# Whole token copies from PSUM, one more pair by seven products, and another order of weight sums in a hybrid decoder layer

## The chip, the cores and the metric

The kernel runs on one core of a Trainium2 chip. A core has a matrix engine (TensorE, PE in the profile), a vector engine (VectorE, DVE), a scalar engine (ScalarE, ACT), GpSimd (POOL) and SyncE (SP, which here issues most transfers). Each engine runs its own instructions in order and waits on semaphores for the others. Matmul results go to PSUM, eight banks of 128 x 512 fp32 each; everything else on the chip is in SBUF. The metric is the device time of one execution in microseconds.

## The reference

One layer works on 512 tokens of width 1024 in fp32: a SwiGLU FFN, a token mixer (two kinds of attention), and a second FFN.

```python
def swiglu(x, w_gate, w_up, w_down):
    return (jax.nn.silu(x @ w_gate) * (x @ w_up)) @ w_down
...
        h = rms_norm(x, ffn1_pre[l])
        x = x + 0.5 * rms_norm(swiglu(h, ffn1_w_gate[l], ffn1_w_up[l], ffn1_w_down[l]), ffn1_post[l])
        h = rms_norm(x, mix_pre[l])
        y = token_mixer(h, w_in[l], nsa_pe_k[l], nsa_w_ck1[l], nsa_w_ck2[l], nsa_pe_v[l],
                        nsa_w_cv1[l], nsa_w_cv2[l], w_nsa_o[l], w_dil_o[l], w_mix_out[l])
        x = x + rms_norm(y, mix_post[l])
        h = rms_norm(x, ffn2_pre[l])
        x = x + 0.5 * rms_norm(swiglu(h, ffn2_w_gate[l], ffn2_w_up[l], ffn2_w_down[l]), ffn2_post[l])
```

The hidden width D_FF is 2816, 22 blocks of 128 columns.

## The kernel before, in words

**Numbers.** Every fp32 operand is kept as two parts, `hi` (ACT casts it to a shorter type, L106) and `lo` (DVE subtracts `hi` from it, L107). A product is three matmuls, hi by hi, hi by lo and lo by hi (`mm3`, L129 to L131).

**An FFN.** The normalised tokens stand transposed, as `xh` and `xl`. The 22 blocks of hidden columns are taken in 11 pairs. A pair is worked in one of two ways. A *classical* pair has four units (gate and up, for two blocks), each of 24 matmuls with 512 columns of tokens; per unit, weights of 128 x 1024 come from DRAM into one of three `raw` buffers and are split. A pair by *seven products* (`strassen`) forms, from the four blocks A11, A12, A21, A22 (gate and up for two halves of the model width), sums S1 to S4 on DVE, splits these, and multiplies them with sums T1 to T4 of the tokens or with blocks of tokens: seven block products, each of 24 matmuls with 256 columns. `STRASSEN` says which pairs go that way: 3 to 10 in the first FFN and 2 to 10 in the second.

**Token sums.** T1 to T4 are formed in `token_sums` while the classical pairs run, a few steps (`STEPS`) behind each block. A step first joins `xh` and `xl` into the whole value again (`join`, L493, DVE), subtracts (L496), and splits the result. Slots of SBUF have tags; a step of work can start when the slot's last user is done.

**The norm.** Token tile t (128 tokens) is scaled by DVE (L197), transposed by PE into two PSUM banks (L202), cast from there by ACT to `xh` (L205), and the rest is taken by DVE to `xl` (L209). `norm_steps` gives these as functions. The banks' tags are given by hand: `OPEN` for the first FFN, `AFTER_MIX` for the second. PSUM has three banks S, two T, one V and two F.

**What sets the order.** The opening (in `run`) is issued by hand, in the order of the text, for ACT, DVE and PE: tile 0 goes through two S banks, tile 1 through two T banks, then the first FFN unit starts. The first four units of an FFN work on the first two tiles alone (256 columns); the first two of them write into banks of tag T ("TTSV"), the others into S and V. `keep_busy` issues transposes of no use to keep PE working. Tiles 2 and 3 are transposed between those units. Elsewhere a scheduler orders each engine's instructions, within what the program's data allow.

Of the kernel before, what the change touches and what calls it, by code (L numbers as in the profile page):

```python
# [12 lines left out]
F32 = mybir.dt.float32  # L13
# [14 lines left out]
NF = DFF // P  # L28
# [31 lines left out]
class Layer:  # L60
    def __init__(self, ctx, tc, a):
        self.tc, self.nc, self.a = tc, tc.nc, a
        self.pool = ctx.enter_context(tc.tile_pool(name="sb", bufs=1))
        self.psum = ctx.enter_context(tc.tile_pool(name="ps", bufs=1, space=PSUM))
        self.nps = 0
        self.consts()

# [118 lines left out]

    def norm_steps(self, t, pre, tags):

        nc = self.nc
        xn = self.sbt("tmp", [P, D], bufs=2)  # L190
        c = slice(t * P, (t + 1) * P)
        xh, xl = self.xht, self.xlt
        pt = {}

        def scale(h, r):
            hc = slice(h * S, (h + 1) * S)
            nc.vector.scalar_tensor_tensor(xn[:, hc], self.x[2 * t + h], r, pre[h], op0=OP.mult, op1=OP.mult)  # L197

        def transpose(h):
            pt[h] = self.bank(tags[h])  # L200
            for j in range(4):
                nc.tensor.transpose(pt[h][:, j * P:(j + 1) * P], xn[:, (4 * h + j) * P:(4 * h + j + 1) * P], self.ident)  # L202
# [73 lines left out]
    def ffn(self, n, wg, wu, wd, post, finish, xsrc, tags, nps, aside=None):  # L276
# [48 lines left out]
        def strassen(p):  # L325
# [17 lines left out]
            r12, r21, r11, r7 = [self.bank() for _ in range(4)]  # L343
            nc.vector.tensor_add(s1, a21, a22)
            w = block(a11)
# [44 lines left out]
        def classical(f, act):  # L390
            bs = []
            for m in "gu":
                if (m, f) in first:
                    w, b = first[m, f]
                    mms(w, b, 2 * P, S)
                else:
                    w = unit(m, f)
                    b = self.bank()
                    mms(w, b, 0, S)
                bs.append(b)  # L400
            nc.scalar.activation(act, bs[0], AF.Silu)
# [69 lines left out]
    def token_sums(self):  # L471


        nc = self.nc
        H = S // 2
        places = []
# [5 lines left out]
        for c in range(2):  # L482
            hi, lo, whole = [[v.rearrange("p (k c) -> p k c", k=2) for v in g]
                             for g in (places[8 * c:8 * c + 4], places[8 * c + 4:8 * c + 8],
                                       [self.slot("x") for _ in range(4)])]
            f1, f2, f3, f4 = whole
# [4 lines left out]
            def join(dst, i, h, c=c):  # L491
                ks, cs = slice(4 * i + 2 * c, 4 * i + 2 * c + 2), slice(h * H, (h + 1) * H)
                nc.vector.tensor_add(dst, self.xht[:, ks, cs].bitcast(F32), self.xlt[:, ks, cs].bitcast(F32))  # L493

# [900 lines left out]
    def run(self, out):  # L1395
# [30 lines left out]
        with self.tc.manual_schedule(engines={ET.Activation, ET.DVE, ET.PE}):  # L1426
# [73 lines left out]
        self.mixer(*boundary(a["mix_post"][0], a["ffn2_pre"][0], self.x2dram, AFTER_MIX))  # L1500
        self.ffn(1, a["ffn2_w_gate"][0], a["ffn2_w_up"][0], a["ffn2_w_down"][0],
# [31 lines left out]
```

## Time and profile before

| | us |
|---|---|
| median of 3 runs | 1138.97 (1138.95 to 1139.98) |
| profiled execution | 1138.51 |
| its span | 1136.4 |
| PE busy | 1119.9 (99%) |
| DVE busy | 908.0 (80%) |
| ACT busy | 638.0 (56%) |
| granted clock of PE, mean | 0.999 |

The span runs from the first to the last instruction that the profiler saw. Busy times are sums over the span; in a window they say how full an engine is there. A row of a timeline gives start, duration, engine, line of the program, operation, output and inputs, and in brackets the time that the engine waited before it and for what.

### The profile page before, as it was taken

Reading aid. Unit: us, or ns where it says so; the run is one execution under the profiler, and the core shown is the slowest. Engines: PE = TensorE matmul, PEld = TensorE weight load, DVE = VectorE, ACT = ScalarE, POOL = GpSimd, SP = SyncE. Lnnn points to the kernel's source line nnn. Section 1 sums busy time; section 2 is a strip of 40 time slices with the busy share of each in tenths; the row PEclk is TensorE's granted clock in tenths of the full one; section 3 lists DMA queues with packets and bytes.
Section 4 is the critical chain, followed back from the end, with each engine's and each line's share of the span. In section 5 each row is a group of like instructions: output and inputs, shape, how many; then the busy total and the mean of one; then the engine's idle time right before and its main releaser. Section 6 shows DMA issues by size and latency. Waiting matters only on the chain.

```text
span 1136.4 us, 18463 instructions
## 1 busy us (share of the span) xinstructions
PE 1119.9 (99%) x6921; PEld 999.5 (88%) x6921; DVE 908.0 (80%) x1563; ACT 638.0 (56%) x1145; POOL 78.3 (7%) x112
## 2 busy tenths in 40 slices
PE   8999999999999999999999999999999999999997
PEld 7889999998878987778888998788989999998885
DVE  6989999878667889687665687976878888979665
ACT  5435555566464688687565635644445555558552
POOL 1000000000022032343000000001000000000001
PEclk9999999999999999999999999999999999999999
DMA  9995665578655552111476758683133433357753
GB/s 321 331 307 187 190 199 186 154 265 295 220 184 148 172 134 85 53 41 56 142 248 224 251 176 293 207 301 107 66 121 121 130 98 129 109 181 236 280 189 115
DMA packets 152908, 206.01 MB, mean 181 GB/s; under 512 B 19794, under 2 KB 97906, under 8 KB 152564
## 3 DMA queue, kind: packets, MB, share of 16 engines
q1 hardware_dynamic: 152816, 204.85, 55.1%
q8 instruction: 54, 0.88, 0.3%
q14 instruction: 34, 0.28, 0.1%
q10 hardware_dynamic: 4, 0.00, 0.0%
HBM read 165.45 MB, written 39.37 MB: 180 GB/s over the span
## 4 chain that ended last, share of the span: by engine, by line
PE 88%; DVE 6%; ACT 2%; DMA 1%; issue 1%; POOL 1%; SPq 0%; POOLq 0%; DVEq 0%; ACTq 0%
PE pb_F L131 11%; PE pb_F L129 11%; PE pb_F L130 11%; PE pb_S L131 8%; PE pb_S L130 8%; PE pb_S L129 8%; PE pb_T L130 6%; PE pb_T L131 6%; PE pb_T L129 6%; PE pb_V L130 3%; PE pb_V L129 3%; PE pb_V L131 3%; PE pb_V L986 2%; PE pb_T L971 1%; DVE SP_s L721 1%
## 5 line engine op out<-in xcount | busy, mean ns | idle before, releaser
L106 ACT CAST whi<-raw 128x1024 fp32r<-128x1024 f32 (+2 forms) x221 | 225.4, 1020 | 260.3 <-issue 68.2
L107 DVE TENSOR_TENSOR wlo<-raw,whi 128x1024 fp32r<-128x1024 f32 (+2 forms) x221 | 261.3, 1185 | 103.6 <-ACT whi L106 99.7
L129 PE MATMUL pb_F<-xh_t,whi 128*128 128x512 f32 (+1 forms) x392 | 142.6, 364 | 0.6 <-ACT whi L106 0.4
L131 PE MATMUL pb_F<-xh_t,wlo 128*128 128x512 f32 (+1 forms) x392 | 141.6, 361 | 0.5 <-DVE wlo L107 0.5
L130 PE MATMUL pb_F<-xl_t,whi 128*128 128x512 f32 (+1 forms) x392 | 141.9, 362 | 0.0
L106 ACT CAST whi<-tmp_t 128x1024 fp32r<-128x1024 f32 x51 | 53.5, 1048 | 61.0 <-PE pb_S L130 22.0
L131 PEld LDWEIGHTS pb_F<-xh_t,wlo 128*128 128x128 f32 x392 | 74.1, 189 | 10.8 <-DVE wlo L107 1.0
L129 PEld LDWEIGHTS pb_F<-xh_t,whi 128*128 128x128 f32 x392 | 74.1, 189 | 10.6 <-ACT whi L106 0.6
L130 PEld LDWEIGHTS pb_F<-xl_t,whi 128*128 128x128 f32 x392 | 74.2, 189 | 9.7
L107 DVE TENSOR_TENSOR wlo<-tmp_t,whi 128x1024 fp32r<-128x1024 f32 x51 | 62.4, 1223 | 25.2 <-ACT whi L106 23.9
L129 PE MATMUL pb_S<-xh_t,whi 128*128 128x256 f32 (+1 forms) x240 | 73.2, 305 | 0.0
L131 PE MATMUL pb_S<-xh_t,wlo 128*128 128x256 f32 (+1 forms) x240 | 73.0, 304 | 0.0
L130 PE MATMUL pb_S<-xl_t,whi 128*128 128x256 f32 (+1 forms) x240 | 73.0, 304 | 0.0
L151 POOL TENSOR_TENSOR rs_t<-rs_t,mhalf_t 128x1 f32<-128x1 f32 x24 | 19.2, 798 | 546.4 <-DVE rs_t L147 546.4
L130 PE MATMUL pb_T<-xl_t,whi 128*128 128x256 f32 (+1 forms) x184 | 53.9, 293 | 0.0
L129 PE MATMUL pb_T<-xh_t,whi 128*128 128x256 f32 (+1 forms) x184 | 53.9, 293 | 0.0
L131 PE MATMUL pb_T<-xh_t,wlo 128*128 128x256 f32 (+1 forms) x184 | 53.8, 292 | 0.0
L962 POOL TENSOR_SCALAR SP_s<-SP_s,st_t 128x384 f32<-128x384 f32 (+2 forms) x48 | 45.7, 968 | 106.5 <-DVE st_t L898 80.5
L130 PEld LDWEIGHTS pb_S<-xl_t,whi 128*128 128x128 f32 x240 | 45.9, 191 | 1.9
L129 PEld LDWEIGHTS pb_S<-xh_t,whi 128*128 128x128 f32 x240 | 45.9, 191 | 1.9
L131 PEld LDWEIGHTS pb_S<-xh_t,wlo 128*128 128x128 f32 x240 | 45.9, 191 | 1.9
L107 DVE TENSOR_TENSOR PT_s<-pb_T,PT_s 128x512 fp32r<-128x512 f32 (+1 forms) x72 | 39.2, 559 | 6.1 <-ACT PT_s L106 5.5
(808 smaller groups left out, 3350.6 us busy)
## 6 DMA issues: line engine op xcount, KB each, us to landing
raw<-in_ffn_w_up_dram SPq DMA_DIRECT2D x36, 512.0 KB, 5.2
raw<-in_w_in_dram SPq DMA_DIRECT2D x18, 1024.0 KB, 5.4
raw<-in_ffn_w_gate_dram SPq DMA_DIRECT2D x35, 512.0 KB, 4.7
raw<-tdram SPq DMA_DIRECT2D x16, 1024.0 KB, 5.2
raw<-in_ffn_w_down_dram SPq DMA_DIRECT2D x14, 1024.0 KB, 5.7
NN_s<-in_ffn_w_down_dram SPq DMA_DIRECT2D x22, 512.0 KB, 5.1
tdram<-NN_s SPq DMA_DIRECT2D x22, 512.0 KB, 3.9
raw<-tdram SPq DMA_DIRECT2D x8, 768.0 KB, 5.9
```

Source lines behind the costliest of these rows:

```text
L106: self.last_cast = self.nc.scalar.copy(dsthi, src).ins
L107: self.last_rest = self.nc.vector.tensor_sub(dstlo, src, dsthi.bitcast(F32)).ins
L129: mm(out, lhi, rhi, start=start, stop=False, skip_group_check=skip)
L130: mm(out, lhi, rlo, start=False, stop=False, skip_group_check=skip)
L131: mm(out, llo, rhi, start=False, stop=stop, skip_group_check=skip)
L151: nc.gpsimd.tensor_tensor(out=r, in0=v, in1=self.mhalf, op=OP.pow)
L721: nc.vector.tensor_tensor_reduce(p, s, w, -1.0, FLOOR, OP.add, OP.min, st_m)
L962: nc.gpsimd.tensor_scalar(pp, pp, st[:, 1, t:t + 1], None, op0=OP.mult)
L971: nc.tensor.transpose(b[:, o + (t - kk) * P:o + (t - kk + 1) * P], pt[pn][:, po + kk * P:po + (kk + 1) * P], self.ident)
L986: self.nc.tensor.matmul(out[:, kk * P:S], v, pp, start=first and kk == 0 and pi == 0, stop=False, skip_group_check=True)
```

## The change

1. At the norm, ACT now also copies each transposed bank whole (`full`, four copies of 128 x 2 x 128 per tile), for the token half 0 into slots V and for half 1 into slots x. `token_sums` reads these; the joins of `xh` and `xl` are gone.
2. Pair 2 of the first FFN is worked by seven products. Token sums are thus spread over blocks 1 to 3 in both FFNs, four steps each.
3. The weight sums of such a pair are formed as S3 = A11 - A21, S2 = A22 - S3, S1 = S2 + A11, S4 = A12 - S2, instead of S1, S3, S2, S4. These are four operations on DVE as before.

```diff
-STRASSEN = range(3, NF // 2), range(2, NF // 2)
+STRASSEN = range(2, NF // 2), range(2, NF // 2)
...
-STEPS = (0, 3, 3, 3, 3), (4, 4, 4)
+STEPS = (0, 4, 4, 4), (0, 4, 4, 4)
...
+WHOLE = "VV", "xx"
...
+    def new_whole(self, half):
+        self.whole[half] = [[self.slot(tag).rearrange("p (k c) -> p k c", k=2) for _ in range(2)] for tag in WHOLE[half]]
...
+        def full(h):
+            if not whole:
+                return
+            if t % 2 == 0 and h == 0:
+                self.new_whole(t // 2)
+            for j in range(2):
+                o = self.whole[t // 2][h][j][:, :, (t % 2) * P:(t % 2 + 1) * P]
+                self.last_cast = nc.scalar.copy(o, pt[h][:, 2 * j * P:2 * (j + 1) * P].rearrange("p (j c) -> p j c", j=2)).ins
...
                 transpose(h)
                 cast(h)
                 rest(h)
+            for h in range(2):
+                full(h)
...
-            nc.vector.tensor_add(s1, a21, a22)
             w = block(a11)
             nc.vector.tensor_sub(a21, a11, a21)
             product(r11, w, b11, True, False)
             w = block(a21)
             product(r7, w, t3, True, True)
-            nc.vector.tensor_sub(s2, s1, a11)
+            nc.vector.tensor_sub(s2, a22, a21)
             w = block(s2)
+            nc.vector.tensor_add(s1, s2, a11)
...
-            if f == 1:
+            if f == 0:
                 sums.extend(self.token_sums())
...
-            def s1(f1=f1, f3=f3, join=join):
-                join(f3, 0, 1)
-                join(f1, 0, 0)
+            def s1(f1=f1, f3=f3):
                 sub(f1, f3, f1)
...
+            full0(0)
             sq2 = self.squares(2)
+            full0(1)
             self.pre_split.append(self.ktiles(self.wsplit(self.pre_raw["g"][:, :, P:2 * P], [KT, P])))
-            t2 = self.norm_T(2, g, OPEN[2], sq2)
+            t2 = self.norm_T(2, g, OPEN[2], sq2, True)
+            full1(0)
             sq3 = self.squares(3)
+            full1(1)
             self.pre_split.append(self.wslots(self.pre_raw["u"][:, :, P:2 * P], "SP"))
-            t3 = self.norm_T(3, g, OPEN[3], sq3)
+            t3 = self.norm_T(3, g, OPEN[3], sq3, True)
```

Two places show how instructions move. First, ACT in the opening, from the split of the second unit's weights (`whi_183`) to that of the fourth's (`SP_s`); `pb_S_136` and `pb_S_142` are tile 0's transposes, `pb_T_155` and `pb_T_166` tile 1's, `whi_201` (`whi_193` before) the third unit's weights, `junk_t` the squares. Before:

```order
L106 CAST whi_183<-raw_83 128x1024
L138 ACTIVATE junk_t_187,ss_t_188<-x_s_78 128x512
L138 ACTIVATE junk_t_190,ss_t_191<-x_s_79 128x512
L106 CAST whi_193<-raw_82 128x1024
L138 ACTIVATE junk_t_204,ss_t_205<-x_s_80 128x512
L138 ACTIVATE junk_t_207,ss_t_208<-x_s_81 128x512
L106 CAST SP_s_210<-raw_83 128x512
```

And of the change:

```order
L109 CAST whi_183<-raw_83 128x1024
L224 COPY V_s_187<-pb_S_136 128x2x128
L224 COPY V_s_188<-pb_S_136 128x2x128
L141 ACTIVATE junk_t_193,ss_t_194<-x_s_78 128x512
L141 ACTIVATE junk_t_196,ss_t_197<-x_s_79 128x512
L224 COPY V_s_189<-pb_S_142 128x2x128
L224 COPY V_s_190<-pb_S_142 128x2x128
L109 CAST whi_201<-raw_82 128x1024
L224 COPY V_s_187<-pb_T_155 128x2x128
L224 COPY V_s_188<-pb_T_155 128x2x128
L141 ACTIVATE junk_t_214,ss_t_215<-x_s_80 128x512
L141 ACTIVATE junk_t_217,ss_t_218<-x_s_81 128x512
```

Six copies stand among these splits and squares; those from `pb_T_155` come ninth and tenth in this list. The other side of it is PE's first FFN unit, whose bank has the same tag T (`pb_T_226` before, `pb_T_238` now), before and now:

```order
L129 MATMUL pb_T_226<-xh_t_88,whi_133 128x256 [waits DVE_49]
```

```order
L132 MATMUL pb_T_238<-xh_t_88,whi_133 128x256 [waits DVE_49,Activation_49]
```

The matmul waits for ACT too. Second, DVE at the start of the second FFN, from tile 3's mean square (`rs_t`) through its scale (`tmp_t`) to the rests of tiles 2 and 3. Before:

```order
L147 TENSOR_SCALAR rs_t<-ss_t 128x1
L197 SCALAR_TENSOR_TENSOR tmp_t<-x_s,rs_t,CP_s 128x512 x2
L209 TENSOR_TENSOR xl_t<-pb_F,xh_t 128x4x128 x2
L209 TENSOR_TENSOR xl_t<-pb_S,xh_t 128x4x128
L209 TENSOR_TENSOR xl_t<-pb_V,xh_t 128x4x128
L493 TENSOR_TENSOR x_s<-xh_t,xl_t 128x512 x3
```

And of the change:

```order
L150 TENSOR_SCALAR rs_t<-ss_t 128x1
L362 TENSOR_TENSOR raw<-raw 128x1024
L203 SCALAR_TENSOR_TENSOR tmp_t<-x_s,rs_t,CP_s 128x512 x2
L215 TENSOR_TENSOR xl_t<-pb_F,xh_t 128x4x128 x2
L215 TENSOR_TENSOR xl_t<-pb_S,xh_t 128x4x128
L215 TENSOR_TENSOR xl_t<-pb_V,xh_t 128x4x128
L507 TENSOR_TENSOR V_s<-x_s,V_s 128x512
```

The sum S3 of a pair's weights (`raw<-raw`) now stands ahead of tile 3's scale, and a subtraction of whole copies stands where the joins stood.

More of the change, by code (lines that the diff above doesn't have):

```diff
@@ L65, in __init__ @@
         self.nps = 0
+        self.whole = {}
         self.consts()
@@ L185, in squares, with norm_steps @@
         return [self.meansq(x, S) for x in self.x[2 * t:2 * t + 2]]
-    def norm_steps(self, t, pre, tags):
+    def new_whole(self, half):
+        self.whole[half] = [[self.slot(tag).rearrange("p (k c) -> p k c", k=2) for _ in range(2)] for tag in WHOLE[half]]
+    def norm_steps(self, t, pre, tags, whole=False):
         nc = self.nc
@@ L209, in rest, with norm_T @@
             self.last_rest = nc.vector.tensor_sub(xl[:, ks, c], pt[h].rearrange("p (j c) -> p j c", j=4), xh[:, ks, c].bitcast(F32)).ins
-        return scale, transpose, cast, rest
-    def norm_T(self, t, pre, tags, sq=None):
+        def full(h):
[6 more added lines that the diff above has]
+                self.last_cast = nc.scalar.copy(o, pt[h][:, 2 * j * P:2 * (j + 1) * P].rearrange("p (j c) -> p j c", j=2)).ins
+        return scale, transpose, cast, rest, full
+    def norm_T(self, t, pre, tags, sq=None, whole=False):
         r = self.rstd(sq or self.squares(t))
-        scale, transpose, cast, rest = self.norm_steps(t, pre, tags)
+        scale, transpose, cast, rest, full = self.norm_steps(t, pre, tags, whole)
         for h in range(2):
@@ L402, in classical @@
             nc.vector.tensor_mul(act, act, bs[1])
-            if f == 1:
+            if f == 0:
                 sums.extend(self.token_sums())
-            if 1 <= f <= len(STEPS[n]):
+            if f < len(STEPS[n]):
                 with self.tc.issue_after(self.last_rest):
-                    for _ in range(STEPS[n][f - 1]):
+                    for _ in range(STEPS[n][f]):
                         sums.pop(0)()
@@ L474, in token_sums @@
         nc = self.nc
-        H = S // 2
         places = []
@@ L482, in token_sums @@
         for c in range(2):
[L483 to L486, printed above, removed]
+            hi, lo = [[v.rearrange("p (k c) -> p k c", k=2) for v in g]
+                      for g in (places[8 * c:8 * c + 4], places[8 * c + 4:8 * c + 8])]
+            whole = f1, f2, f3, f4 = [self.whole[h][i][c] for i, h in ((0, 0), (1, 1), (0, 1), (1, 0))]
             for i in range(4):
@@ L489, in token_sums @@
                     o.extend(v[:, k] for k in range(2))
-            def join(dst, i, h, c=c):
-                ks, cs = slice(4 * i + 2 * c, 4 * i + 2 * c + 2), slice(h * H, (h + 1) * H)
-                nc.vector.tensor_add(dst, self.xht[:, ks, cs].bitcast(F32), self.xlt[:, ks, cs].bitcast(F32))
             def sub(dst, x, y):
@@ L499, in parts, with s2, s3 @@
                 self.split(hi[i], lo[i], whole[i])
-            def s1(f1=f1, f3=f3, join=join):
-                join(f3, 0, 1)
-                join(f1, 0, 0)
+            def s1(f1=f1, f3=f3):
                 sub(f1, f3, f1)
-            def s2(f1=f1, f2=f2, f3=f3, join=join):
-                join(f2, 1, 1)
+            def s2(f1=f1, f2=f2, f3=f3):
                 sub(f3, f2, f3)
                 sub(f2, f2, f1)
-            def s3(f2=f2, f4=f4, join=join):
-                join(f4, 1, 0)
+            def s3(f2=f2, f4=f4):
                 sub(f4, f4, f2)
@@ L1440, in run @@
             r0 = self.rstd(sq0)
-            scale0, transpose0, cast0, rest0 = self.norm_steps(0, g, OPEN[0])
-            scale1, transpose1, cast1, rest1 = self.norm_steps(1, g, OPEN[1])
+            scale0, transpose0, cast0, rest0, full0 = self.norm_steps(0, g, OPEN[0], True)
+            scale1, transpose1, cast1, rest1, full1 = self.norm_steps(1, g, OPEN[1], True)
             hi, lo = self.wpair([KT, P])
@@ L1475, in run, with boundary @@
             self.pre_split = [self.ktiles(w) for w in ((hi, lo), self.wsplit(self.pre_raw["u"][:, :, 0:P], [KT, P]))]
+            full0(0)
             sq2 = self.squares(2)
+            full0(1)
             self.pre_split.append(self.ktiles(self.wsplit(self.pre_raw["g"][:, :, P:2 * P], [KT, P])))
-            t2 = self.norm_T(2, g, OPEN[2], sq2)
+            t2 = self.norm_T(2, g, OPEN[2], sq2, True)
+            full1(0)
             sq3 = self.squares(3)
+            full1(1)
             self.pre_split.append(self.wslots(self.pre_raw["u"][:, :, P:2 * P], "SP"))
-            t3 = self.norm_T(3, g, OPEN[3], sq3)
+            t3 = self.norm_T(3, g, OPEN[3], sq3, True)
         self.pending = [t2, t3]
-        def boundary(post, pre, store, tags=None):
+        def boundary(post, pre, store, tags=None, whole=False):
             def load():
@@ L1494, in finish @@
                         self.new_xT()
-                    self.pending.append(self.norm_T(t, gain, tags[t]))
+                    self.pending.append(self.norm_T(t, gain, tags[t], None, whole))
             return load, finish
@@ L1499, in run @@
                  *boundary(a["ffn1_post"][0], a["mix_pre"][0], self.xdram, AFTER_FFN), a["x"][0], "TTSV", 6, self.distances)
-        self.mixer(*boundary(a["mix_post"][0], a["ffn2_pre"][0], self.x2dram, AFTER_MIX))
+        self.mixer(*boundary(a["mix_post"][0], a["ffn2_pre"][0], self.x2dram, AFTER_MIX, True))
         self.ffn(1, a["ffn2_w_gate"][0], a["ffn2_w_up"][0], a["ffn2_w_down"][0],
```

## The prediction

> **What bounds the kernel now.** I read the busy times and the chain of waits first, then busy time by windows over the two FFNs, then TensorE's (PE's) timeline with ScalarE (ACT) and VectorE (DVE) beside it where the diff changes something.
>
> ```profile
> PE 1119.9 (99%) x6921; PEld 999.5 (88%) x6921; DVE 908.0 (80%) x1563; ACT 638.0 (56%) x1145; POOL 78.3 (7%) x112
> ...
> PE 88%; DVE 6%; ACT 2%; DMA 1%; issue 1%; POOL 1%; SPq 0%; POOLq 0%; DVEq 0%; ACTq 0%
> ```
>
> ```profile
> core 0: us, PE busy (x) PEld busy (x) DVE busy (x) ACT busy (x) POOL busy (x), PEclk, DMA share, GB/s
> 12.00:337.00 325.00, 323.91 (x2155) 298.85 (x2154) 280.23 (x370) 175.99 (x255) 6.20 (x14) 1.00 0.71 236
> 780.00:1117.00 337.00, 336.61 (x2299) 312.86 (x2297) 273.31 (x351) 185.00 (x273) 5.41 (x9) 1.00 0.45 149
> ```
>
> PE fills the span, and within the FFNs it misses only 1.09 of 325.00 us and 0.39 of 337.00. So an edit there pays only if PE issues less, and costs only if PE comes to a stop. DVE at 86% of the first window (280.23 of 325.00) is next. My sum has three questions: what the new products save on PE, where a new order stops PE, and whether the clock holds.
>
> **Pair 2 by seven products.** PE's timeline, start and duration of each row:
>
> ```profile
> 76.32 0.39 PE L129 MATMUL pb_V<-xh_t,whi 128*128 128x512 f32 x1
> 81.76 0.28 PE L129 MATMUL pb_S<-xh_t,whi 128*128 128x256 f32 x1
> ...
> 104.79 0.28 PE L129 MATMUL pb_V<-NN_s,whi 128*128 128x256 f32 x1
> 107.67 0.28 PE L129 MATMUL pb_S<-NN_s,whi 128*128 128x256 f32 x1
> ```
>
> The first two rows are the last classical unit of pair 2 and the start of pair 3: 81.76 - 76.32 = 5.44 us for 24 matmuls of 512 columns, 0.227 each. The other two bound one block product: 107.67 - 104.79 = 2.88 us for 24 of 256 columns, 0.12 each. A classical pair is four units, 4 x 5.44 = 21.76; the new one 7 x 2.88 = 20.16. **Saving 1.60 us**: an eighth less work would be 2.72, but 256 columns take 0.12 where half of 0.227 would be 0.114, and 168 x 0.0067 gives 1.1 of it back. Nothing else in the change takes work from PE, so 1.60 us is also all that it can gain.
>
> **The opening: who may write the T banks.** At the start, the first two FFN units write the two T banks of PSUM, which hold tile 1's transposed tokens. Until now these were free once ACT had cast them to xh and DVE had taken xl. Now ACT must copy from them first, and in its order the two copies from the first T bank stand behind two from S, the squares of tile 2, two more from S and the split of a third unit's weights. The issue order shows the new wait on ACT at the first of PE's 256-column matmuls. Rows of before:
>
> ```profile
> 11.43 0.60 PE L1424 MATMUL pb_V<-ident_t 128*128 128x128 f32 x4
> 12.03 0.39 PE L129 MATMUL pb_T<-xh_t,whi 128*128 128x256 f32 x1
> ```
>
> ```profile
> 12.14 1.06 ACT L106 CAST whi<-raw 128x1024 fp32r<-128x1024 f32 x1
> 13.10 0.64 ACT L138 ACTIVATE junk_t<-x_s 128x512 bf16<-128x512 f32 x1
> ...
> 13.86 0.63 ACT L138 ACTIVATE junk_t<-x_s 128x512 bf16<-128x512 f32 x1
> ...
> 15.04 1.05 ACT L106 CAST whi<-raw 128x1024 fp32r<-128x1024 f32 x1 [0.46 <-DMA raw<-in_ffn_w_gate_dram]
> 15.99 0.62 ACT L138 ACTIVATE junk_t<-x_s 128x512 bf16<-128x512 f32 x1
> ```
>
> The copy itself isn't in the trace; the nearest row, ACT out of PSUM with the same 128x256, is this group (busy 11.5 us, mean 370 ns):
>
> ```profile
> L106 ACT CAST PT_s<-pb_T 128x256 fp32r<-128x256 f32 x32 | 11.5, 370 | 7.3 <-DVE PT_s L107 3.8 <-PE pb_T L1237 2.3 <-PE pb_T L971 1.0
> ```
>
> Neighbours on ACT overlap by some 0.1 us: the cast of 1.06 is followed 0.96 later, the square of 0.63 (with its accumulator read) 0.76 later. So a copy advances ACT by 0.28 when another follows. The chain: split 12.14 to 13.10; two copies to 13.66; two squares (0.76 each) to 15.18; two copies to 15.74; the split of 0.95 to 16.69 (its DMA had landed by 15.04); two copies, the last in full, 16.69 + 0.28 + 0.37 = 17.34. With a handover of 0.06, PE's first FFN matmul moves **from 12.03 to about 17.40**. If copies didn't overlap at all (0.37 each), it is 17.85; at 0.22 each 17.1.
>
> The second T bank comes free two squares and two copies later, 17.25 + 1.52 + 0.65 = 19.42; the second unit wants it at 17.40 + 2.88 = 20.28, so it adds no wait. What follows swallows part of the delay:
>
> ```profile
> 18.93 1.31 PE L202 MATMUL pb_S<-ident_t,tmp_t 128*128 128x128 f32 x8 [0.65 <-DVE tmp_t L197]
> ...
> 22.95 1.04 PE L202 MATMUL pb_F<-ident_t,tmp_t 128*128 128x128 f32 x8
> 23.74 0.36 PE L129 MATMUL pb_V<-xh_t,SP_s 128*128 128x256 f32 x1
> ...
> 26.69 0.28 PE L129 MATMUL pb_T<-xh_t,whi 128*128 128x256 f32 x1
> ```
>
> Two units 17.40 + 5.76 = 23.16; tile 2's eight transposes at the 0.79 of the third and second row (23.74 - 22.95), the third unit at 2.95 (26.69 - 23.74), then tile 3's transposes and the fourth unit the same: 23.16 + 2 x (0.79 + 2.95) = 30.64, where 26.69 stood. The opening costs **+3.95 us** (3.6 to 4.4 by the two copy prices); the 0.65 of waiting in the first row is gone, since the scaled tokens are then long there.
>
> **The start of the second FFN.** No bank wait there: AFTER_MIX frees both T banks before units reach them. But in DVE's order a weight sum of 128x1024 (now S3) goes between tile 3's mean square and its scale:
>
> ```profile
> 800.19 0.21 DVE L147 TENSOR_SCALAR rs_t<-ss_t 128x1 f32<-128x1 f32 x1 [0.95 <-ACT junk_t L138]
> 801.13 1.41 DVE L197 SCALAR_TENSOR_TENSOR tmp_t<-x_s,rs_t,CP_s 128x512 f32<-128x512 f32 x2 [0.73 <-POOL rs_t L151]
> ```
>
> ```profile
> 802.03 0.60 PE L202 MATMUL pb_S<-ident_t,tmp_t 128*128 128x128 f32 x4
> 802.60 0.66 PE L202 MATMUL pb_V<-ident_t,tmp_t 128*128 128x128 f32 x4
> ```
>
> DVE sat idle for 0.73 of that; the sum takes about 1.13 (1.22 for one of its size in the row at 73.20 below, less the 0.1 by which neighbours overlap), so it starts at about 800.4 and ends near 801.5, and the scale, PE's transposes behind it and the units behind those come **+0.35 us** later (0, if the order on the chip lets the sum fall elsewhere, to 0.5).
>
> **DVE elsewhere, costed at nothing.** The joins that go are these:
>
> ```profile
> L493 DVE TENSOR_TENSOR x_s<-xh_t,xl_t x16: 681/684/687, 34.9 to 828.8; 128x512 f32<-128x512 f32 x16
> ```
>
> Eight per FFN at some 0.60 spacing leave DVE 4.8 us. A Strassen pair, though, asks more of it than a classical one:
>
> ```profile
> 38.20:60.00 21.80, 21.80 (x99) 18.04 (x97) 21.06 (x35) 6.96 (x10) 1.44 (x2) 1.00 0.90 303
> 60.00:81.80 21.80, 21.80 (x98) 18.06 (x97) 18.14 (x26) 7.49 (x11) 0.00 (x0) 1.00 0.93 313
> 101.90:122.10 20.20, 20.20 (x171) 20.20 (x170) 19.28 (x26) 10.93 (x15) 0.00 (x0) 1.00 0.62 203
> 73.20 1.22 DVE L344 TENSOR_TENSOR tmp_t<-raw 128x1024 f32<-128x1024 f32 x1 [2.00 <-DMA raw<-in_ffn_w_up_dram]
> ```
>
> DVE is busy 19.28 of 20.20 us in such a pair, yet PE is busy for all 20.20. Token sums that were spread over pairs 0 to 2 must now be done by the end of pair 1, in the 21.80 us from 38.20 where DVE already works 21.06; but the joins' 4.8 us go from there, and PE's 4 us of delay in the opening add room before it. ACT has 7 to 11 us of work in each of these windows; 32 copies of 0.28, 9 us over both FFNs, fit. The cover is DVE's lead over PE; without it, each us that DVE is late is a us of PE. The order S3, S2, S1, S4 has four operations like the old; no Strassen pair of before shows PE waiting for a sum, so nothing is there to win. ACT and SP have no other long queue moved past them: V slots come later to the early loads of pair 5, x slots earlier to pairs 3 and 4.
>
> **Sum at full clock:** 1138.51 (the profiled execution; span 1136.4 and 2.1 around it) - 1.60 + 3.95 + 0.35 = 1141.2. The timed runs have their median at 1138.97, 0.46 above the profiled one; measured the same way, that is 1141.7.
>
> **The clock.** PE now idles for 17.40 - 12.03, about 5.4 us. What idling did to the granted clock in this trace shows only at its ends:
>
> ```profile
> 1129.56 0.39 PE L131 MATMUL pb_T<-whi,PT_s 128*128 128x512 f32 x1
> ```
>
> ```profile
> 1133.50:1134.00 0.50, 0.00 (x0) 0.00 (x0) 0.00 (x0) 0.00 (x0) 0.00 (x0) 1.00 0.98 360
> 1134.00:1134.20 0.20, 0.00 (x0) 0.00 (x0) 0.00 (x0) 0.00 (x0) 0.00 (x0) 0.78 1.17 430
> 1134.20:1134.40 0.20, 0.00 (x0) 0.00 (x0) 0.00 (x0) 0.00 (x0) 0.00 (x0) 0.50 0.93 358
> ```
>
> ```profile
> 6.69 1.97 PE L202 MATMUL pb_S<-ident_t,tmp_t 128*128 128x128 f32 x8 [0.41 <-DVE tmp_t L197]
> ...
> 10.42 0.64 PE L1424 MATMUL pb_V<-ident_t 128*128 128x128 f32 x2
> 10.85 0.75 PE L202 MATMUL pb_T<-ident_t,tmp_t 128*128 128x128 f32 x4
> ```
>
> After the last matmul (1129.56 + 0.39 = 1129.95) the clock fell to 0.50 at about 1134.1, 4.2 us later. At the start, two transposes took 0.43 (10.85 - 10.42), 0.215 each, where eight take 0.79 in the row at 22.95, 0.099 each: PE ran at half speed until about 11, 4.3 us after the dense work of 6.69 had begun. A gap of 5.4 us is longer than 4.2, so I take it that PE comes back at half speed and keeps it for up to 4.3 us, in which half the work is lost: 0 to 2.1 us. I take 0.9, below the middle, since the gap passes 4.2 by only 1.2 and the three timed runs need not all be hit: **1142.6**.
>
> The Trainium skill, "TensorE: Matmul & The Clock Gate" (Part 1: The HAM clock gate), says that the gate halves the clock after an idle window of about 3.4 us and restores it after about as much sustained work, with windows that run freely whatever the kernel does. The 4.2 us at the end agree with that. By windows that don't start with the gap, 5.4 us can hold a whole one or not; the page thus speaks for a time that varies between executions, and by its 3.4 us an estimate of the loss would be 1.7 us or none.
>
> **Rivals.**
> (a) The clock stays full: the gap holds no complete stretch that the gate counts. For it: only 1.2 us separate the gap from the 4.2 that it took. From rows alone, the rise near 11 and the fall at 1134.1 are places of such a rhythm, and what lies between them is unknown. Then 1141.7. Chance 0.30. That is the case to which the page's free-running window belongs.
> (b) The banks come free early, and PE starts by about 12.3 as before: ACT would have to come to T's copies ahead of the squares and the splits. ACT works 12.14 to 15.99 with no idle but 0.46, and the order shows the wait, so little speaks for it. Then 1138.97 - 1.60 + 0.35 = 1137.7, not slower. It decides if the first copy out of T starts before 12.3. Chance 0.06.
> (c) DVE's lead is too short: in order as it is, it waits for a weight load (the 2.00 us at 73.20 is one), with the new pair's operands and the token sums queued behind; PE then stops in pair 1 or 2. The same 2.00 us once more on top of the forecast gives 1144.6. Against it: joins gone, and the opening's delay gives DVE 4 us. Chance 0.10.
> The forecast (PE late, half clock for a while) has 0.54.
>
> **How the numbers follow.** A change under 0.2%, 2.28 us here, can't be told from none. The forecast, 1142.6 (1141.2 to 1144.3 by 3.6 to 4.4 in the opening, 0 to 0.5 in the second FFN and 0 to 2.1 of clock, not all at one end), is slower than 1141.25 for nearly all of it: 0.52 of 0.54. Of (a), 0.45 us above that bound, 0.20 of 0.30. (b) is within the bound but for 0.02. (c) is slower. Slower 0.52 + 0.20 + 0.10 = 0.82; same 0.02 + 0.10 + 0.04 = 0.16; faster 0.02. The range, with (a)'s lower half and (c) in it: 1140.6 to 1145.0.
>
> **What would show it.** Right: PE's first 128x256 matmul into pb_T starts at 17.1 to 17.9, released by ACT's copy out of pb_T; transposes of tile 2 follow the second unit without a wait; its 256-column matmuls are 0.2 us or more apart for some us and then 0.12, or 0.12 from the start (a). Pair 2 lasts 20.2 us, with PE filled from 31 to the end of pair 3. Tile 3's scale in the second FFN is 0.3 to 0.4 later in relation to its mean square. Wrong: an FFN start by 12.3; a PE wait for a wlo of 1 us or more in pairs 0 to 3; or a window with the FFN's PE under 99%.

## The result, and the profile after

The changed kernel takes 1149.58 us (median of 4 runs, 1147.91 to 1151.4) against 1139.22 for the kernel before (1138.95 to 1139.98): a ratio of **1.009, interval 1.0075 to 1.0104**, 10.4 us slower. The way was forecast (0.82 for slower), the size was not: 1142.6 in a range to 1145.0. Its profiled execution took 1147.91 us with a span of 1146.1. Of the kernel before, one run beside the first batch below (the change with parts undone) took 2211.0 us and is left out, and one beside the second (one part at a time, and the copies with banks V, S, T, T) took 1154.49 us at a granted clock of 0.927, where its others took 1138.7 to 1141.5, so the intervals of that batch are wide; medians are compared there.

The page of the changed kernel, its busy times and the chain that ended last:

```profile
PE 1121.8 (98%) x6993; PEld 1004.3 (88%) x6993; DVE 906.4 (79%) x1557; ACT 651.6 (57%) x1185; POOL 79.4 (7%) x112
...
PE 76%; DVE 11%; DMA 5%; issue 3%; ACT 3%; POOL 1%; SPq 0%; DVEq 0%; POOLq 0%; ACTq 0%
```

PE does only 1.9 us more work than before, but its share of the chain fell from 88% to 76%; VectorE and transfers took it over. What PE waited for, by line (total, times, longest):

```profile
PE pb_T L132 <- ACT V_s L224: 4.7, 1, 4.7
PE pb_S L1279 <- DVE PT_s L110: 2.2, 2, 1.7
...
PE pb_S L134 <- DVE wlo L110: 0.7, 2, 0.4
```

The first row is the bank wait of the opening. The others are short, and a list by length hides them; they are found by laying the two traces side by side. Both end with the same matmuls, so PE's rows can be counted back from the last one, and the start of each compared. In the table, "+4.71" means that this matmul starts 4.71 us later in its span than the same one before. The columns are places of the kernel before: pair 3's start (81.8 us), the last pairs of the first FFN (214.8), two places around the end of the mixer (704.7 and 746), the second FFN once all tiles are transposed (816.9), and the last matmul.

| run (one profiled execution each) | 81.8 | 214.8 | 704.7 | 746 | 816.9 | last | median of the timed runs, us |
|---|---|---|---|---|---|---|---|
| the change | +4.71 | +7.04 | +7.35 | +8.64 | +9.52 | +9.49 | 1149.58 |
| old sums | +4.37 | +4.38 | +3.89 | +5.31 | +5.36 | +5.39 | 1143.54 |
| banks V, S, T, T | -1.10 | +1.12 | +1.43 | +1.83 | +2.66 | +2.66 | 1141.40 |
| dummies | +3.27 | +5.36 | +5.47 | +5.69 | +6.52 | +6.51 | 1144.84 |
| both edits | -0.99 | -0.98 | -1.36 | -1.34 | -1.31 | -1.27 | 1139.76 |
| before, new sums only | +0.15 | +2.57 | +3.04 | +3.41 | +4.28 | +4.26 | 1141.79 |
| before, pair 2 only | +2.29 | +2.29 | +2.12 | +2.70 | +2.72 | +2.76 | 1143.67 |
| before, copies only | +5.34 | +5.34 | +5.49 | +5.77 | +5.81 | +5.82 | 1144.95 |
| both edits, fewer sums | +0.17 | +0.18 | +0.12 | +0.98 | +1.06 | +1.06 | 1138.72 |
| both edits, four sums on GpSimd | +8.30 | +8.31 | +7.84 | +8.85 | +8.89 | +9.01 | 1148.40 |
| both edits, fewer loads | -0.72 | -0.72 | -1.11 | -0.56 | -0.52 | -0.48 | 1137.38 |
| copies, banks V, S, T, T | -0.17 | -0.17 | +0.27 | +0.29 | +0.33 | +0.37 | 1138.67 |
| both edits, late call | +0.83 | +2.07 | +1.74 | +3.68 | +3.93 | +3.93 | 1139.79 |
| copies, banks V, S, T, T, late call | -0.85 | -0.85 | -0.51 | -0.25 | -0.07 | +0.32 | 1138.49 |

The change's own row reads as a sum. At pair 2's start it is +6.32; pair 2 takes 1.61 off; pairs 3 to 9 add 2.33, of it 1.53 in pair 3; the mixer 1.60, most of it at one place near 710 us; the start of the second FFN 0.88. That place in the mixer differs from run to run (0.0 to 1.9 us between the columns 704.7 and 746, and both ends of that are kernels with the same banks and the same sums, "both edits" without and with the late call): VectorE waits there for a transfer, of the change and of the kernel before:

```profile
717.19 1.23 DVE L110 TENSOR_TENSOR wlo<-raw,whi 128x1024 fp32r<-128x1024 f32 x1 [1.61 <-DMA NN_s<-in_ffn_w_down_dram]
```

```profile
708.58 1.23 DVE L107 TENSOR_TENSOR wlo<-raw,whi 128x1024 fp32r<-128x1024 f32 x1 [0.35 <-DMA NN_s<-in_ffn_w_down_dram]
```

I don't count it to the change; that it has another cause is not shown, since each kernel has one profile.

**The opening.** PE's timeline of the changed kernel, to be held against 12.03 before:

```profile
11.89 1.06 PE L1431 MATMUL pb_V<-ident_t 128*128 128x128 f32 x4
17.66 0.58 PE L132 MATMUL pb_T<-xh_t,whi 128*128 128x256 f32 x1 [4.71 <-ACT V_s L224]
18.04 0.41 PE L133 MATMUL pb_T<-xl_t,whi 128*128 128x256 f32 x1
18.26 0.41 PE L134 MATMUL pb_T<-xh_t,wlo 128*128 128x256 f32 x1
...
22.10 0.35 PE L134 MATMUL pb_T<-xh_t,wlo 128*128 128x256 f32 x1
22.29 0.28 PE L132 MATMUL pb_T<-xh_t,whi 128*128 128x256 f32 x1
22.41 0.28 PE L133 MATMUL pb_T<-xl_t,whi 128*128 128x256 f32 x1
...
25.52 1.04 PE L208 MATMUL pb_S<-ident_t,tmp_t 128*128 128x128 f32 x8
```

ScalarE at the same time:

```profile
13.56 0.65 ACT L224 COPY V_s<-pb_S 128x256 f32<-128x256 f32 x2
14.09 0.65 ACT L141 ACTIVATE junk_t<-x_s 128x512 bf16<-128x512 f32 x1
...
16.01 1.05 ACT L109 CAST whi<-raw 128x1024 fp32r<-128x1024 f32 x1
16.95 0.66 ACT L224 COPY V_s<-pb_T 128x256 f32<-128x256 f32 x2
17.48 0.66 ACT L141 ACTIVATE junk_t<-x_s 128x512 bf16<-128x512 f32 x1
```

The chain is the forecast one, each copy 0.26 behind the last: the two copies from the first T bank end at 16.95 + 0.66 = 17.61, and PE starts at 17.66, released by them. Then its matmuls are 0.213 apart (22 from 17.66 to 22.10) until 22.1, and 0.12 from 22.29 on. In this run the half speed didn't begin in the gap: the four transposes just ahead of it took 1.06 us (11.89), where before they took 0.60 (11.43), so PE hadn't come to full speed yet. Its clock record begins with full speed at 22.25, where that of the kernel before begins at 11.13; ahead of the first entry the profile counts full speed, whatever the spacing. The second T bank causes no wait, nor do tile 2's transposes.

**VectorE in the pairs.** Two neighbours on VectorE, and PE behind them:

```profile
90.75 1.22 DVE L362 TENSOR_TENSOR raw<-raw 128x1024 f32<-128x1024 f32 x1 [2.63 <-DMA raw<-in_ffn_w_up_dram]
91.90 1.22 DVE L110 TENSOR_TENSOR wlo<-tmp_t,whi 128x1024 fp32r<-128x1024 f32 x1
```

```profile
93.17 0.39 PE L134 MATMUL pb_F<-NN_s,wlo 128*128 128x256 f32 x1 [0.54 <-DVE wlo L110]
```

The first is S3 of pair 4 (L362), a pair that PE begins only at 108.2. It waits 2.63 us for its weights. Behind it, in order, stands a split of pair 3, which PE needs at once. So the new sum, early because it needs only one half of the next pair's weights, holds up a split that has all its data.

**The second FFN's start.** VectorE and GpSimd of the changed kernel:

```profile
808.87 0.22 DVE L150 TENSOR_SCALAR rs_t<-ss_t 128x1 f32<-128x1 f32 x1 [0.95 <-ACT junk_t L141]
809.02 1.23 DVE L362 TENSOR_TENSOR raw<-raw 128x1024 f32<-128x1024 f32 x1
810.68 1.41 DVE L203 SCALAR_TENSOR_TENSOR tmp_t<-x_s,rs_t,CP_s 128x512 f32<-128x512 f32 x2 [0.44 <-POOL rs_t L154]
```

```profile
809.23 1.42 POOL L154 TENSOR_TENSOR rs_t<-rs_t,mhalf_t 128x1 f32<-128x1 f32 x1 [2.75 <-DVE rs_t L150]
```

GpSimd's step in the kernel before:

```profile
800.55 0.55 POOL L151 TENSOR_TENSOR rs_t<-rs_t,mhalf_t 128x1 f32<-128x1 f32 x1 [2.75 <-DVE rs_t L147]
```

And PE of the changed kernel:

```profile
811.49 0.66 PE L208 MATMUL pb_S<-ident_t,tmp_t 128*128 128x128 f32 x4 [0.65 <-DVE tmp_t L203]
```

The scale starts 1.81 us after its mean square, 0.94 before. The sum ends at 810.25, so it isn't what the scale waits for: it waits for GpSimd's root of one column, which takes 1.42 us beside the sum, for 0.55 before. So it is in every profile of the table: 1.40 to 1.42 with the new sums (the change, banks V, S, T, T, dummies, new sums only), 0.55 with the old ones.

### The profile page after: what moved, and what is told of

Its sections match the earlier page's. It is cut to its first block, busy times and chain, and to the rows that moved or that the text cites. A ratio compares the mean times of both kernels' runs of the same rounds, so it can differ in the third digit from the quotient of the medians.

```text
span 1146.1 us, 18653 instructions
## 1 busy us (share of the span) xinstructions
PE 1121.8 (98%) x6993; PEld 1004.3 (88%) x6993; DVE 906.4 (79%) x1557; ACT 651.6 (57%) x1185; POOL 79.4 (7%) x112
## 4 chain that ended last, share of the span: by engine, by line
PE 76%; DVE 11%; DMA 5%; issue 3%; ACT 3%; POOL 1%; SPq 0%; DVEq 0%; POOLq 0%; ACTq 0%
PE pb_F L134 10%; PE pb_F L132 10%; PE pb_F L133 10%; PE pb_S L134 6%; PE pb_S L132 6%; PE pb_S L133 6%; PE pb_T L133 5%; PE pb_T L134 5%; PE pb_T L132 5%; DVE wlo L110 2%; PE pb_V L133 2%; PE pb_V L132 2%; PE pb_V L134 2%; PE pb_V L993 2%; DMA raw<-in_ffn_w_up_dram 2%
## 5 line engine op out<-in xcount | busy, mean ns | idle before, releaser
L109 ACT CAST whi<-tmp_t 128x1024 fp32r<-128x1024 f32 x54 | 56.7, 1050 | 53.3 <-PE pb_S L133 19.9
L110 DVE TENSOR_TENSOR wlo<-tmp_t,whi 128x1024 fp32r<-128x1024 f32 x54 | 65.9, 1221 | 22.0 <-ACT whi L109 21.6
L132 PE MATMUL pb_T<-xh_t,whi 128*128 128x256 f32 x184 | 53.1, 289 | 4.7 <-ACT V_s L224 4.7
L134 PE MATMUL pb_T<-xh_t,wlo 128*128 128x256 f32 x184 | 53.0, 288 | 0.0
L133 PE MATMUL pb_T<-xl_t,whi 128*128 128x256 f32 x184 | 53.0, 288 | 0.0
```

The lines of the kernel that those rows point to most:

```text
L109: self.last_cast = self.nc.scalar.copy(dsthi, src).ins
L110: self.last_rest = self.nc.vector.tensor_sub(dstlo, src, dsthi.bitcast(F32)).ins
L132: mm(out, lhi, rhi, start=start, stop=False, skip_group_check=skip)
L133: mm(out, lhi, rlo, start=False, stop=False, skip_group_check=skip)
L134: mm(out, llo, rhi, start=False, stop=stop, skip_group_check=skip)
```

## The experiments

**Undo the order of sums.**

```diff
+            nc.vector.tensor_add(s1, a21, a22)
             w = block(a11)
             nc.vector.tensor_sub(a21, a11, a21)
...
-            nc.vector.tensor_sub(s2, a22, a21)
+            nc.vector.tensor_sub(s2, s1, a11)
             w = block(s2)
-            nc.vector.tensor_add(s1, s2, a11)
```

> The changed kernel with the weight sums in the old order (S1, S3, S2, S4); everything else as changed. Theory A (the new order lets S3 of the next pair stand ahead of the current pair's last splits on VectorE, where it waits for its weights' transfer): the waits of VectorE on raw weights ahead of S3 go, PE's stops in pairs 3 to 9 (2.3 us in the changed kernel's profile) and the 0.9 us ahead of tile 3 in the second FFN go too: 1149.6 - 3.2 = 1146.4 us. Rival B (VectorE simply has too much to do once pair 2 is taken by seven products, whatever the order): the stops stay, 1149 to 1150 us.

Measured 1143.54 us, 6.0 less than the changed kernel (ratio to before 1.0043, 1.0028 to 1.0058). From pair 3 to pair 9 nothing is lost any more (+4.37, +4.38), and nothing at the second FFN's start (+5.31, +5.36). VectorE's waits between 80 and 230 us, first of the change, then of this run:

```profile
DVE raw L362 <- DMA raw<-in_ffn_w_up_dram: 5.3, 4, 2.6
```

```profile
DVE wlo L110 <- ACT whi L109: 5.8, 9, 1.0
```

Theory A holds and B falls. In the profiles the two places give the 3.2 us that were expected; the median fell by 2.8 us more, and that part no trace shows.

**Other banks for the first units.**

```diff
-... a["x"][0], "TTSV", 6, self.distances)
+... a["x"][0], "VSTT", 6, self.distances)
```

> The changed kernel with the first four FFN units on banks V, S, T, T instead of T, T, S, V, so that the first two need no bank that ScalarE still copies from. Theory A (the opening's loss is the bank wait and the half clock behind it): PE's first FFN matmul goes back to about 12 us, at 0.12 us spacing soon after, and 6.3 us go: 1149.6 - 6.3 = 1143.3 us. Rival C (the late opening was cover for VectorE, whose waits in pairs 0 to 3 now reach PE): 2 to 4 us come back, about 1146 us.

Measured 1141.40 us, 8.2 less than the change (1.0021, 1.0011 to 1.0032). PE:

```profile
11.23 0.60 PE L1431 MATMUL pb_V<-ident_t 128*128 128x128 f32 x4
11.98 0.36 PE L132 MATMUL pb_V<-xh_t,whi 128*128 128x256 f32 x1
12.18 0.28 PE L133 MATMUL pb_V<-xl_t,whi 128*128 128x256 f32 x1
```

The bank wait is gone, with the clock's part: +4.71 became -1.10 at pair 3. The later losses of the change stay (2.2 and 0.83), so the late opening did not cause them. Pair 2 starts 0.62 earlier than before, but it lasts 21.28 us instead of the change's 20.15: PE stops in it, and 1.1 of its 1.6 us are lost. That much of rival C is there.

**Dummies in the gap.**

```diff
+            keep_busy(36)
             full0(0)
```

> The changed kernel with 36 more transposes of no use on PE, put into the gap ahead of the first FFN unit, so that PE is busy while it waits for the bank. Theory A (21 matmuls behind the gap run at half clock, 0.213 instead of 0.12 us each): the start stays near 17.7 us, the spacing is 0.12 from there, and 2.0 us go: 1147.6 us, and the spread between runs is smaller. Rival D (the wide spacing comes from something other than the clock, operands or banks): spacing and time stay, 1149.6 us.

Measured 1144.84 us, 4.7 less than the change (1.0055, 1.0038 to 1.0072). PE:

```profile
10.93 4.53 PE L1431 MATMUL pb_V<-ident_t 128*128 128x128 f32 x40
16.86 0.39 PE L132 MATMUL pb_T<-xh_t,whi 128*128 128x256 f32 x1 [1.41 <-ACT V_s L224]
17.09 0.28 PE L133 MATMUL pb_T<-xl_t,whi 128*128 128x256 f32 x1
17.20 0.27 PE L134 MATMUL pb_T<-xh_t,wlo 128*128 128x256 f32 x1
```

The bank still comes free late (16.86, for 17.66 in the change), but PE comes out of the wait at 0.12 a matmul: the wide spacing was the clock. Pair 2 starts 2.83 us earlier than in the change, 0.80 by the earlier start and 2.0 by the clock, as theory A has it; pair 2 itself takes 1.4 of that back (21.53 us). The spread didn't shrink (1143.83 to 1146.95). In the run with old sums, where PE waits as long (4.79 us), the clock was full ahead of the gap, and the windows show the grant itself:

```profile
12.20:15.40 3.20, 0.03 (x1) 0.00 (x0) 2.25 (x3) 3.17 (x10) 0.00 (x0) 1.00 1.21 301
15.60:17.00 1.40, 0.00 (x0) 0.00 (x0) 0.55 (x1) 1.40 (x4) 0.00 (x0) 0.50 1.03 399
17.00:22.30 5.30, 5.28 (x25) 5.28 (x26) 3.97 (x8) 2.88 (x8) 1.57 (x3) 0.50 1.05 382
22.40:30.00 7.60, 7.60 (x67) 7.60 (x66) 2.15 (x4) 2.76 (x7) 0.15 (x1) 1.00 1.10 349
```

PE is idle from 12.2, the clock is half from about 15.4, and full again only at 22.3, 5.3 us after PE had come back at 17.02.

**Both edits.** 

> Both edits: first units on banks V, S, T, T, and the old order of weight sums. Theory A (the two losses are separate and add): 1149.6 - 6.3 - 3.2 = 1140.1 us, within 0.2% of the kernel before. Rival B/C (VectorE is the bound once the opening is no longer late): 1143 us or more.

Measured 1139.76 us (1137.09 to 1146.79; ratio 1.0011, 0.9994 to 1.0029): the level of the kernel before, as expected, but with a spread of 9.7 us. Its profile, of the fastest run, ends 1.27 us ahead of before, and neither place costs anything in it. So the new banks and the old sums take back 9.8 of the 10.4 us; the spread asks for another cause, below. The granted clock of the runs goes with it: 0.998 or 0.999 in the four up to 1138.65 us, 0.997 in the three to 1140.86, 0.996 in the three above.

**One part at a time, put into the kernel before.** The new sums alone, pair 2 alone (with joins; token sums in blocks 1 to 3), and the copies alone:

```diff
-STRASSEN = range(3, NF // 2), range(2, NF // 2)
-STEPS = (0, 3, 3, 3, 3), (4, 4, 4)
+STRASSEN = range(2, NF // 2), range(2, NF // 2)
+STEPS = (4, 4, 4), (4, 4, 4)
```

> The kernel before with the new order of weight sums alone (S3, S2, S1, S4); joins, classical pair 2 and the opening as before. Theory A (S3 of the next pair stands too early on VectorE and waits there for its weights): VectorE waits on raw weights ahead of S3 again, PE stops in the first FFN's Strassen pairs, and tile 3's scale in the second FFN comes late: 0.9 us there and 1 to 2.5 us in the first FFN, 1139.3 + 2 to 3.4 = 1141.3 to 1142.7 us. Rival (the order hurts only together with pair 2 and the copies): only the 0.9 us of the second FFN, 1140.2 us, or nothing.

> The kernel before with pair 2 of the first FFN by seven products and the token sums, with their joins, over three blocks; old opening, old sums. Theory A' (the saving is real, but the weights of pairs 2 and 3 come late on a full DMA, so that PE stops there by 0 to 3 us, other in each execution): 1139.3 - 1.6 + 1 = 1138.7 us with a spread of several us. Rival (VectorE has no room for the joins there): 2 us or more slower than before in all executions, 1141 us or more.

> The changed kernel with classical pair 2 and the old order of weight sums, so that only the whole copies are left, in the opening too. Theory A: the opening's loss alone, 6.0 to 6.3 us in a profile: 1139.3 + 6.2 = 1145.5 us. Rival (part of that loss needs the other edits): under 1143 us.

The sums alone: 1141.79 us, 2.4 over before (1.0011, 0.9982 to 1.0039); the profile shows the losses at their two places, 2.42 and 0.87, and VectorE waits for S3's weights as in the change:

```profile
DVE raw L345 <- DMA raw<-in_ffn_w_up_dram: 8.4, 5, 2.6
```

The copies alone: 1144.95 us, 5.6 over (1.0037, 1.0011 to 1.0064); +5.34 at pair 3, and then little. Both are as theory A has it. Pair 2 alone was a surprise: 1143.67 us, 4.3 *over* before, from 1141.13 to 1146.82 (1.0031, 1.0002 to 1.0059). PE in the profile:

```profile
65.29 0.39 PE L129 MATMUL pb_V<-NN_s,whi 128*128 128x256 f32 x1 [1.68 <-ACT whi L106]
66.81 0.38 PE L129 MATMUL pb_S<-NN_s,whi 128*128 128x256 f32 x1 [1.01 <-ACT whi L106]
```

With stops before and in pair 2 it is +2.29 at pair 3, where -1.6 was due. The rival's price is met, and in this profile VectorE has no room: it works without a break from 56.1 to 70.3 us, and PE's stop up to 65.29 ends when ACT has cast the weight sum that VectorE finishes at 64.15. A window of this run, columns as in the prediction's:

```profile
60.00:82.00 22.00, 19.31 (x155) 18.74 (x154) 21.93 (x27) 10.92 (x14) 0.00 (x0) 1.00 0.94 309
```

VectorE is busy for 21.93 of 22.00 us; in the run with both edits, which has no joins, for 18.93. The granted clock, 0.999 in the fastest run, is 0.994 in the slowest. The three parts alone add up to 12.3 us by medians, more than the 10.4 of the change, and there the saving of pair 2 exists: from copies alone (1144.95) to old sums, which is copies and pair 2 (1143.54), it is 1.4 us. When the opening is 6 us late, VectorE and the transfers have 6 us more; that this is why, is argued and not shown.

**Copies without the bank wait.** The run of the copies alone with banks V, S, T, T.

> The copies alone as in the run before, with the first four units on banks V, S, T, T: what the copies are worth without the bank wait. Theory A: nothing on the way to the end changes, 1139.3 + 0.6 (opening, by the run with both edits) = 1139.9 us, and, since pair 2 is classical, with the small spread of the kernel before. Rival G (the wide spread of the run with both edits comes from the copies or the banks, not from pair 2): the spread stays at 5 us or more.

Measured 1138.67 us (0.9984, 0.9957 to 1.0011), nine of ten runs from 1138.11 to 1140.01 and one at 1141.03. The copies cost nothing when no one waits for their banks, and with classical pair 2 the spread is narrow: G falls, and the spread of both edits belongs to pair 2.

**What makes pair 2 late?** Three runs on the kernel with both edits, on the down weights' sums of pairs 9 and 10 that are made early, in pairs 1 and 0. The first leaves the subtractions out, the second puts those for pair 9 on GpSimd, the third leaves the loads out.

```diff
-            self.nc.vector.tensor_sub(out, x, y)
+            (engine or self.nc.vector).tensor_sub(out, x, y)
...
-                    self.early_sums(AHEAD[p], wd, [...])
+                    self.early_sums(AHEAD[p], wd, [...], self.nc.gpsimd if p else None)
```

> The run with both edits (banks V, S, T, T and old sums; 1139.8 us, 1137 to 1147), but the eight subtractions of 128x512 on VectorE for the down weights of pairs 9 and 10, issued in pairs 0 and 1 of the first FFN, are left out, so that these sums are not computed; their loads and stores stay. Theory V (pair 2's saving is lost because VectorE is full in pairs 0 to 2, and SyncE's queue, with the weights behind stores that wait for VectorE, falls late): 4.8 us of VectorE less, PE's stops near 74 us go, 1137.1 us or less with a spread under 2 us. Rival M (the transfers themselves are too many for the time): stops and spread stay, 1139 to 1140 us.

> The run with both edits, with the four subtractions for pair 9 (issued in pair 1) on GpSimd instead of VectorE; nothing is left out. Theory V: 2.4 us less on VectorE where it is fullest; the median falls to 1137.5 to 1138.5 us and the spread shrinks; it would beat the kernel before by 1 us or so. Rival M: 1139 to 1140 us with the wide spread; a slowing of VectorE by GpSimd's accesses would show as longer VectorE instructions and 1140 us or more.

> The run with both edits, but the 2 MB of loads for the down weights of pairs 9 and 10 in pairs 0 and 1 are left out (GpSimd writes zeros into their places instead, so these weights count as zero); VectorE's subtractions and the stores stay. Theory V: VectorE is as full as before, so PE's stops and the spread stay, 1139 to 1140 us. Rival M: with 2 MB less before 75 us (some 7 us of transfers at 300 GB/s) the weights land early, and it is 1137 us with a spread under 2 us.

Without the subtractions: 1138.72 us (1137.33 to 1140.62; 0.9998, 0.9989 to 1.0007), and PE still stops in pair 2, up to 63.77 and 67.43 us for 0.8 us each. Without the loads: 1137.38 us (1135.81 to 1139.20; 0.9979, 0.9970 to 0.9988), and PE doesn't stop in the pairs. With GpSimd: 1148.40 us (1.0076, 1.0062 to 1.0090), the opposite of what was hoped. PE, the window behind its stop, GpSimd (by its line: durations in ns, least, middle and greatest, then first and last start in us), VectorE at that time, and SyncE of that run:

```profile
69.62 0.58 PE L132 MATMUL pb_V<-NN_s,whi 128*128 128x256 f32 x1 [7.00 <-ACT whi L109]
```

```profile
69.60:74.50 4.90, 3.61 (x15) 3.32 (x16) 4.90 (x8) 3.03 (x4) 0.00 (x0) 0.50 0.83 234
```

```profile
L465 POOL TENSOR_TENSOR KB_s<-KB_s x4: 1615/1620/2013, 47.3 to 52.8; 128x512 f32<-128x512 f32 x4
```

```profile
48.10 1.78 DVE L465 TENSOR_TENSOR raw<-raw 128x512 f32<-128x512 f32 x1
```

```profile
51.05 3.72 SPq L476 DMA_DIRECT2D tdram<-KB_s  x2
54.87 0.38 SPq L329 DMA_DIRECT2D tdram<-raw  x1
55.30 0.45 SPq L476 DMA_DIRECT2D tdram<-KB_s  x1
55.80 2.53 SPq L352 DMA_DIRECT2D raw<-in_ffn_w_up_dram  x2
```

The four subtractions, 1.6 to 2.0 us each, keep GpSimd from 47.3 to 54.4 us. The stores of their results stand on SyncE's queue ahead of pair 2's weights, so these are issued at 55.8 and later, and PE stops for 7 us. Behind the stop the clock is half until 74.5, and pair 2 lasts 30.5 us instead of 20.15: 8.3 of waits and some 2 of slow matmuls. The sign that was named for a slowing of VectorE by GpSimd is there too: four of its operations of 128x512 take 1.77 or 1.78 us each while GpSimd works, for 0.68 elsewhere. PE's stop doesn't come from that, since VectorE then waits 7.10 us for the weights. Less work on VectorE helped by 1.0 us, less to load by 2.4, and either brought the spread from 9.7 to 3.3 or 3.4; rival M's prediction is nearest. But the loads that the third run leaves out also held SyncE's queue (the four for pair 9 from 39.1 to 44.3 us in the run with both edits), so it doesn't tell how much must land from what stands ahead of the weights.

**The queue's order alone.** The call for a pair's down weights moves from the middle of a seven-product pair to its end, with pair 2 by seven products and with the classical one.

```diff
-            weight_sums(p)
             act = [self.slot("ring") for _ in range(2)]
...
             nc.vector.tensor_mul(act[1], act[1], up[1])
+            weight_sums(p)
             return act
```

> The run with both edits (banks V, S, T, T and old sums; 1139.8 us), with the call that loads, sums and stores a pair's down weights moved from the middle of a seven-product pair to its end; nothing is left out. SyncE's order then has both halves of pair 3's weights ahead of the four stores that wait for VectorE's sums. Theory Q (pair 2's saving is lost because the next weights stand behind those loads and stores on SyncE's queue): PE's stops between 62 and 76 us go, 1137 to 1137.8 us in nearly all executions, better than the kernel before. Rival M (the amount of transfers before 75 us decides, whatever their order): 1139 to 1140 us with a spread of several us as before.

> The same with classical pair 2, that is the copies with banks V, S, T, T alone (1138.7 us) and the late call. No PE stop is there to remove: 1138.7 us again by theory Q and by rival M. It is the partner of the run with seven products in pair 2: their difference is what pair 2 is worth, 1.0 to 1.6 us by Q, none or a loss by M.

Measured 1139.79 us (1137.47 to 1143.21; 1.0007, 0.9998 to 1.0015) and 1138.49 us (1137.71 to 1139.60; 0.9992, 0.9984 to 1.0001). Pair 2 is worth nothing in that order either; it costs 1.3, and in the profile PE stops for 2.28 us up to 76.97. But the order was changed for less than intended:

```profile
65.47 1.63 SPq L471 DMA_DIRECT2D KB_s<-in_ffn_w_down_dram  x2
67.14 0.98 SPq L352 DMA_DIRECT2D raw<-in_ffn_w_up_dram  x2
```

```profile
74.55 1.23 DVE L361 TENSOR_TENSOR tmp_t<-raw 128x1024 f32<-128x1024 f32 x1 [4.94 <-DMA raw<-in_ffn_w_up_dram]
```

The first weights of pair 3 still stand behind pair 2's loads, and from their issue at 67.14 to VectorE's use at 74.55 it is 7.4 us. Whether a better order would do without fewer transfers stays open.

The best version is the copies with banks V, S, T, T, classical pair 2, old sums: 1138.67 and, with the late call, 1138.49 us. Both lie 0.6 to 0.7 us under the kernel before by median, with intervals that reach it.

## Why the prediction was wrong

- **The bank wait** was right as a mechanism and nearly so in size: start at 17.66 for 17.40, and no second wait. Rival (b) fell.
- **The clock** was right in its effect and mis-sized: 0.9 was taken out of "0 to 2.1". In the profile it is 21 matmuls by 0.213 - 0.12, 2.0 us. With the start 0.26 later, the opening costs +6.32 where 3.95 + 0.9 = 4.85 stood. I had treated the half clock as something that ends 4.3 us after PE's return at the latest; in the run with old sums it took 5.3. That run, and the copies alone, show the fall within the gap that I had assumed; in the change's profile PE came into the gap at half speed already. The Trainium skill, "TensorE: Matmul & The Clock Gate" (Part 1: The HAM clock gate), has windows of 3413 ns that run freely and asks for a busy one; the clock record of that run agrees, with half speed for 6.8 us, two windows. By such windows PE came back (17.02) inside one, and the next had to pass before the clock rose at 22.3, so that half speed can outlast PE's return by more than one window. Filling the gap was worth 4.7 us by medians, but 3.0 between the profiled runs (1147.91 and 1144.93); the rest is not explained.
- **"The order S3, S2, S1, S4 ... nothing is there to win"** is the step that failed. The term was zero in the first FFN and 0.35 in the second; it is 2.33 and 0.88 in the profile, and 2.4 (alone) to 6.0 us (undone) by medians. Without it, in the run with old sums, the time is 1143.54 us, below the range's end of 1145.0. I compared the number of operations and asked whether PE waits for a sum. The question that I left out was what stands behind the sum on VectorE: S3 needs one of the two weight buffers of the next pair where S1 needed both, so it is put earlier, and waits in front of a split. I did use that rule for the second FFN's start, and not for the pairs.
- **The second FFN's start**: the sum does delay the scale, but not by its own time after the mean square (which would be 0.35); it delays GpSimd's step (1.42 for 0.55). The Trainium skill, "SBUF — State Buffer" (SBUF: two separate sides), says that VectorE, when it reads two inputs from SBUF, and GpSimd lock one port pair against each other for a whole instruction. The trace agrees: GpSimd's step starts 0.21 behind the sum's start and ends 0.40 behind its end.
- **Pair 2's saving** of 1.60 was right in the change (1.61), where the late opening left time for its weights. As the text had it, with "DVE's lead" as cover, it would have failed without that: alone it costs 4.3 us. Rival (c) named a weight load that VectorE waits for. In the change that is what holds up pair 3, by the new sums, while pairs 1 and 2 run without a stop; with the opening in time it is found in pair 2 as well, and with the joins VectorE itself is full there.
- **The range** ended at 1145.0. Profile against profile, the forecast 1142.6 - 0.46 and the measured 1147.91 are 5.8 apart: the opening's 1.5, the sums' 2.9 and the mixer's 1.6 make 6.0. The timed runs of the changed kernel lie 1.4 to 3.5 us over its profiled one, where I had added 0.46. Their granted clock on record is 0.994 or 0.995, for 0.998 in the profiled one, but the latter counts the half speed ahead of 22.25 as full (it reads 1.00 where matmuls are 0.213 apart), so the two can't be turned into microseconds; what these runs lose besides isn't in a trace.

## What to carry to other kernels

A new reader of a buffer is a new release condition for whoever writes it next: look for the engine order around that reader, and, where the bound engine stops for some us, price the slow clock after the stop too. An operation that needs fewer inputs isn't free: an in-order engine may come to it earlier and wait there, with ready work behind it. A saving on the bound engine needs its operands sooner, so ask whether transfers and their queue can deliver before counting it.

## What the runs showed of the hardware that was not expected

Three profiles show the clock fall at a stop of PE: 4.8 us with old sums, 5.2 with the copies only, 7.0 with the subtractions on GpSimd. In each the clock was half for 6.8 us, and full again only 5.3, 4.1 and 4.9 us after PE had come back. A GpSimd step on a single column took 1.40 to 1.42 us instead of 0.55 where VectorE subtracted two inputs of 1024 columns at the same time. A subtraction of 128x512 on GpSimd took 1.62 us, and once 2.01, with VectorE at work beside it, where VectorE takes 0.68; VectorE's own operations of that size took 1.78 meanwhile.
